# Retention values (first half) and attention values (second half) projected 512 columns at a time, with weights partly in the attention's buffers

## The chip, the cores and the metric

The kernel runs on one core of one Trainium2 chip. The metric is the device time of the core in microseconds (us), taken as the median of several runs of the compiled program. A second source is the profile of one execution: when each instruction of each engine started and ended, and what it waited for. The engines are TensorE (PE, with its weight loads as PEld), VectorE (DVE), ScalarE (ACT), GpSimd (POOL) and SyncE (SP), whose queue issues all the DMAs of this kernel.

## The reference, cut to what matters

One layer of a streaming encoder. Every row of x (2048 prompt rows and 64 sample rows, 1024 wide) is normalised and multiplied by one wide input weight, whose columns are cut into ten pieces:

```
h = rmsnorm(x, norm_g) @ w_in
qa, ka, va, za, qb, kb, vb, zb, ga, gb = jnp.split(h, _split_points(), axis=-1)
...
oa = diff_attn_prompt(qa, ka, va, lam, slopes)
ob, r_p = retention_prompt(qb, kb, vb, log_g)
...
oa = rmsnorm(oa, subln_g) * (1 - lam_init) * silu(za)
ob = rmsnorm(ob) * silu(zb)
m = sigmoid(ga + b_gate[0]) * (oa @ w_oa) + sigmoid(gb + b_gate[1]) * (ob @ w_ob)
y = x + m @ w_out
```

All of it is float32. `va` (attention values) and `vb` (retention values) are 512 columns each, as are `ka`, `qa`, `kb`, `qb`, `za`, `zb`; `ga` and `gb` are 1024 each. `va` is also an output. The sample rows attend to 4096 cached frames besides their own.

## The kernel before, in words

**Precision.** TensorE works on a rounded float32. Every operand is split into a high and a low part (`h` by an ACT cast, line 504, `l` by a subtraction, line 514), and a product is the sum of three matmuls: high by high, high by low, low by high (`mm_group`, line 554). So one 128-row tile of x against one piece of weights is 8 chunks of the contraction by 3 matmuls, 24 in all. The 64 sample rows go through line 550 with 16.

**Two halves.** The prompt's 2048 rows are worked on in two halves of 1024 rows (8 tiles of 128); the sample's 64 rows go with the first half. In each half a stream of projections runs, called W below (`w_stream`, from line 2072), over the column pieces in an order written out by hand. There are three forms:

- *Narrow* (`natural`, line 628): x is stationary, 256 columns of weights move. Two row tiles share one PSUM bank of 512 columns (tag `mm`, two banks). A 512-column piece takes two such passes, g = 0 and g = 1.
- *Wide* (`natural` with `wide`): x is stationary, 512 columns of weights move, one row tile fills a bank. Before the change the first half's `va`, `ka` and `qa` are wide, in this order.
- *Transposed* (`transposed`): weights are stationary and x moves. All of `qb`, `kb`, `za`, `zb`, `ga`, `gb`, in both halves.

In the first half before the change: wide `va`, `ka`, `qa`, then narrow `vb` (two passes), then the transposed pieces. In the second half (`ORD`, line 2237): narrow `va` g 0, `ka` g 0, `qa` g 0, a mark, `va` g 1, `ka` g 1, `qa` g 1, a mark, then narrow `vb` and the transposed pieces.

**Eviction.** `fin_va` (line 763) scales the bank by the rows' norms on ACT (line 786), splits it, and stores high part, low part and output. `fin_vb` (line 815) scales it on ACT (line 827) and stores it. `fin_qk` normalises, transposes (line 734) and stores queries and keys. All go to scratch in DRAM, from which attention and retention load them.

**Weight rooms.** A weight piece is loaded into one of three staging buffers (`ws`), cast and subtracted into two rooms, `wh` and `wl` (`w_room`, line 470; `w_piece`; `w_low`). Narrow pieces use the 12 `w` rooms, two each. Before the change, wide pass 0 (`va`) and wide pass 2 (`qa`) use the attention's buffers `K` and `V` (four of each; one `K` and one `V` hold two of a pass's eight pieces), and wide pass 1 (`ka`) uses the `w` rooms and the two `q` buffers. A room comes free when the last tile of its pass has used it.

**The attention side**, called Z below (`z_stream`): for each half and each of four heads, `load_head` takes `K` and `V` buffers (two of each per head in the first half, four of each in the second) and loads keys and values; `attn_head` and `qk_block` do the scores (lines 1052 and 1053), softmax, transposes (line 1160) and values (lines 1138 to 1140). After the first half's heads come the sample's attention (lines 1221 to 1420) and eight blocks of retention (lines 1486 to 1563); in the second half four blocks follow head 2 and four follow head 3.

**What sets the order.** The program is written by a planner: tasks with priorities and a model of each engine's time decide the order of instructions on PE, ACT, DVE and POOL, which is then fixed; the DMAs on SP are ordered by the framework. Z has priority, and W fills the time in which Z waits. Z of a half may start when the mark `kqv0` (then 0 or 1 for the half) is set: in the first half after the wide `qa`, in the second after `qa` g 0, so with only half of `va`. Heads 2 and 3 wait for `kqv1`.

**The output stage.** When Z is done, `out_prep` loads the branches' output weights, `zaT`, `oaT`, `zbT`, `obT` and gates for the first of eight groups, then for the next (`og_fin`, high and low parts by lines 1677 and 1680). When W is done, the output matmuls begin: eight groups of 8 tiles by 24 matmuls (`m_tile`, lines 1722 to 1724), then the last projection (line 1934), for which `b_prep` loads `w_out`.

Of the kernel before, what the change touches and what calls it, by code (L numbers as in the profile page):

```python
# [8 lines left out]
F32 = mybir.dt.float32  # L9
# [50 lines left out]
class Hybrid:  # L60
# [434 lines left out]
    def w_piece(self, wait):  # L495
# [9 lines left out]
        th = self.A(512, max(self.pe, t))  # L505
        return self.w_low(wide, n, st, h, l, th, tag, tags)

    def w_low(self, wide, n, st, h, l, t, tag, tags):
        th = t
        if n == 1:  # L510
            self.nc.vector.tensor_sub(l, st, h.bitcast(F32))
# [250 lines left out]

    def fin_va(self, g, nh=2):
        nc = self.nc
        ep = self.ep
        hs = slice(2 * g, 2 * g + nh)

        def fin(ps, r, nu, t0, t, bank="mm"):
            n, rt = 128 * nh * nu, r * nu
            rs, eps = yield from self.roots(t0)  # L770
            home = "ev" if nh < 4 or r < 128 else "ath" if t0 // 128 % 2 else "atl"
            yield from self.take(home)
            if nh == 4:
                yield from self.take("row")
                both = self.row("vhl").bitcast(F32R)
                hi, lo = both[:r, :512], both[:r, 512:]
            else:
                yield from self.take("thi")
                yield from self.take("tlo")
                hi = self.sb(ep, [128, 512], "thi", dt=F32R)[:r, :n]  # L780
                lo = self.sb(ep, [128, 512], "tlo", dt=F32R)[:r, :n]
            raw = self.sb(ep if home == "ev" else self.ap, [128, 512], home, "raw")[:r, :n]
            w = 128 * nh
# [6 lines left out]
            t1 = self.A(n, t2)  # L790
            nc.vector.tensor_sub(lo, raw, hi.bitcast(F32))
            t3 = self.V(n, t1)
            if t0 < T:
                dst = self.o["v_prompt"][0, 0, t0:t0 + rt, hs]
            else:
                dst = self.o["v_sample"][0, 0, :, hs]
            yield t1
            gsl = slice(256 * g, 256 * g + 128 * nh)
            th = self.rows_out(self.vN[0][t0:t0 + rt, gsl], hi.bitcast(F32), nu, nh << 16)
            if nh < 4:  # L800
                self.give("thi", th)
            yield t2
            td = self.rows_out(dst.rearrange("t h e -> t (h e)"), raw, nu, nh << 16)
            if t0 == T:
                td = self.st(self.vsN[:, gsl], raw, 1 << 16)
            self.give(home, td)
            yield t3
            tl = self.rows_out(self.vN[1][t0:t0 + rt, gsl], lo.bitcast(F32), nu, nh << 16)
            if nh < 4:
# [6 lines left out]
    def fin_vb(self, g):  # L816
        nc = self.nc
        ep = self.ep

        def fin(ps, r, nu, t0, t, bank="mm"):  # L820
            n, rt = 256 * nu, r * nu
            rs, eps = yield from self.roots(t0)
            yield from self.take("ev")
            raw = self.sb(ep, [128, 512], "ev", "raw")[:r, :n]
            for u in range(nu):
                sl = slice(256 * u, 256 * u + 256)
                nc.scalar.activation(raw[:, sl], ps[:, sl], AF.Identity, scale=rs[:r, u:u + 1])
                t = self.A(256, t, 60)
            self.give(bank, t)
            yield t  # L830
            self.give("ev", self.rows_out(self.vbN[t0:t0 + rt, 256 * g:256 * g + 256], raw, nu, 1 << 17))

# [125 lines left out]
    def load_head(self, half, h):  # L958
# [1113 lines left out]
    def w_stream(self):  # L2072
        self.wq = []
        qa, ka, va, za, qb, kb, vb, zb, ga, gb = range(0, 5120, 512)
        gb = 5120
        fva = [(va + 256 * g, lambda half, g=g, f=f: self.natural(half, self.fin_va(g), f))
               for g in range(2) for f in (True, False)]
        fva, fva0 = fva[1::2], fva[0]
# [8 lines left out]
        for g in range(2):  # L2087
            seq.append((vb + 256 * g, lambda half, g=g: self.natural(half, self.fin_vb(g))))
        for base, dst, n, sc in ((qb, self.qbT, 2, None), (kb, self.kbT, 2, KB_SCALE)):
# [9 lines left out]
        seqs = [f + seq for f in first]  # L2099
        self.order = [[(c[0], len(c) > 2) for c in q if c[0] is not None] for q in seqs]  # L2100
# [10 lines left out]
        for half in range(2):  # L2111
            for k, (c0, f, *_) in enumerate(seqs[half]):
                if c0 is None:
                    self.spawn(self.mark(f"{f}{half}"), 0)
                else:
                    yield from f(half)
                if half == 0 and c0 == vb + 256:
                    self.give("row", self.pe)
# [24 lines left out]
    def z_stream(self):  # L2143
        for half in range(2):
            yield lambda: f"kqv0{half}" in self.done
            if half == 0:
# [89 lines left out]

def ORD(va0, va, k, q, m0, m1):
    return [va0, k[0], q[0], m0, va[1], k[1], q[1], m1]

# [56 lines left out]
```

## Time and profile before

| | |
|---|---|
| median of 3 runs | 1945.42 us (1945.01 to 1947.52) |
| the profiled execution | 1945.82 us, span of its instructions 1944.0 us |
| TensorE clock granted, mean | 0.998 of full |
| PE, PEld busy | 1927.5 us, 1731.2 us |
| DVE, ACT, POOL busy | 1166.6 us, 964.9 us, 490.1 us |
| DMA | 303.32 MB, mean 156 GB/s |
| first half's wide and narrow passes | from the start to 230 us |
| attention scores, first half and second half | 189.8 to 388.1 us and 876.8 to 1441.7 us |
| last matmul of W, first of the output stage | about 1575 us |

The span is the time from the first to the last instruction; the execution's own time is 1.8 us more. A matmul's duration in the trace overlaps the next matmul's, so the rate of a run of matmuls is read from the distance of their starts: the chain of waits gives such runs as start, length and count. "Idle" stands in the trace for time in which an engine had nothing running, with what ended it.

### The profile page before, as it was taken

How to read it: one execution, taken by the hardware profiler on the slowest of the kernel's cores; microseconds unless marked ns; L12 is line 12 of the kernel's file. 1: busy time of each engine (PE TensorE's matmuls, PEld its weight loads, DVE VectorE, ACT ScalarE, POOL GpSimd, SP SyncE). 2: the span in 40 equal slices, each digit the busy share in tenths (PEclk: the TensorE clock that was granted, in tenths of full speed). 3: DMA queues.
4: the chain of work that ended last, by engine and by line, in shares of the span. 5: the costliest groups of instructions: out<-in, count | busy, mean ns of one | idle time of the engine just before them, and what ended most of it. 6: DMA issues, size and time to landing. Idle time of an engine off the chain costs nothing.

```text
span 1944.0 us, 33842 instructions
## 1 busy us (share of the span) xinstructions
PE 1927.5 (99%) x11984; PEld 1731.2 (89%) x11984; DVE 1166.6 (60%) x2798; ACT 964.9 (50%) x2072; POOL 490.1 (25%) x429
## 2 busy tenths in 40 slices
PE   9999999999999999999999999999999999999999
PEld 8779999999988899999998888888888889998887
DVE  6753777646666336648856757845773376545643
ACT  7443766544434235535765646544563445653321
POOL 4310112112122121211121111112113356543422
PEclk9999999999999999999999999999999999999999
DMA  7747454335566655654344253363133678866651
GB/s 235 240 151 199 143 143 132 106 102 156 163 192 187 166 148 168 202 183 141 112 120 128 76 146 96 99 185 116 63 99 108 190 229 259 264 196 189 190 151 65
DMA packets 372074, 303.32 MB, mean 156 GB/s; under 512 B 77440, under 2 KB 334720, under 8 KB 371904
## 3 DMA queue, kind: packets, MB, share of 16 engines
q1 hardware_dynamic: 371904, 301.16, 52.6%
q8 instruction: 94, 1.54, 0.4%
q14 instruction: 76, 0.62, 0.1%
HBM read 195.87 MB, written 100.14 MB: 152 GB/s over the span
## 4 chain that ended last, share of the span: by engine, by line
PE 88%; DVE 5%; DMA 3%; POOL 1%; issue 1%; ACT 1%; SPq 1%; DVEq 0%; POOLq 0%; ACTq 0%
PE mm L554 51%; PE mm L1934 4%; PE s L1052 3%; PE s L1053 3%; PE at L1160 3%; PE at L1934 2%; PE pv L1139 2%; PE pv L1140 2%; PE pv L1138 2%; PE s L1934 1%; PE s L1723 1%; PE s L1724 1%; PE pv L1521 1%; PE mm L1723 1%; PE s L1722 1%
## 5 line engine op out<-in xcount | busy, mean ns | idle before, releaser
L514 POOL TENSOR_TENSOR wl<-ws,wh 128x512 fp32r<-128x512 f32 x191 | 261.4, 1380 | 896.2 <-ACT wh L504 544.9
L554 PE MATMUL mm<-xh,wh 128*128 128x512 f32 (+2 forms) x1280 | 460.7, 360 | 0.0
L554 PE MATMUL mm<-xh,wl 128*128 128x512 f32 (+2 forms) x1280 | 452.7, 354 | 0.0
L554 PE MATMUL mm<-xl,wh 128*128 128x512 f32 (+2 forms) x1280 | 451.9, 353 | 0.0
L554 PEld LDWEIGHTS mm<-xh,wl 128*128 128x128 f32 x1280 | 241.0, 188 | 31.7
L554 PEld LDWEIGHTS mm<-xh,wh 128*128 128x128 f32 x1280 | 241.4, 189 | 29.1 <-issue 0.2
L554 PEld LDWEIGHTS mm<-xl,wh 128*128 128x128 f32 x1280 | 241.6, 189 | 27.8
L554 PE MATMUL mm<-wh,xh 128*128 128x256 f32 (+1 forms) x768 | 236.7, 308 | 0.0
L554 PE MATMUL mm<-wh,xl 128*128 128x256 f32 (+1 forms) x768 | 231.3, 301 | 0.0
L554 PE MATMUL mm<-wl,xh 128*128 128x256 f32 (+1 forms) x768 | 231.0, 301 | 0.0
L1175 DVE TENSOR_TENSOR atl<-at,ath 128x512 fp32r<-128x512 f32 (+1 forms) x144 | 93.7, 659 | 136.2 <-ACT ath L1173 136.1
L504 ACT CAST wh<-ws 128x512 fp32r<-128x512 f32 x192 | 117.0, 617 | 112.6 <-PE mm L554 90.3
L1091 ACT ACTIVATE row<-row,a_mx 128x1024 f32<-128x1024 f32 (+7 forms) x160 | 153.7, 962 | 24.5 <-DVE a_mx L1071 24.3
L554 PEld LDWEIGHTS mm<-wh,xh 128*128 128x128 f32 x768 | 146.3, 190 | 7.1 <-issue 0.5
L554 PEld LDWEIGHTS mm<-wl,xh 128*128 128x128 f32 x768 | 146.4, 191 | 6.7 <-issue 0.5
L554 PEld LDWEIGHTS mm<-wh,xl 128*128 128x128 f32 x768 | 146.3, 190 | 5.5
L865 DVE TENSOR_TENSOR ev<-mm,rsb 128x512 f32<-128x512 f32 x140 | 83.0, 593 | 112.8 <-PE mm L554 112.4
L1173 ACT CAST ath<-at 128x512 fp32r<-128x512 f32 (+1 forms) x144 | 78.7, 563 | 141.5 <-PE at L1160 138.4
L1061 DVE CUSTOM_DVE_ANT_0 row<-s,dfar 128x512 f32<-128x512 f32 (+2 forms) x192 | 118.2, 630 | 46.4 <-PE s L1053 45.9
L1052 PE MATMUL s<-K,q 128*128 128x512 f32 (+3 forms) x320 | 118.4, 374 | 0.7 <-DVE a_acc L1061 0.7
L1053 PE MATMUL s<-K,q 128*128 128x512 f32 (+3 forms) x320 | 115.2, 362 | 0.0
L1110 ACT ACTIVATE row<-row,a_w 128x1024 f32<-128x1024 f32 (+4 forms) x96 | 85.1, 898 | 34.4 <-DVE a_w L1105 31.2
(342 smaller groups left out, 4193.5 us busy)
## 6 DMA issues: line engine op xcount, KB each, us to landing
ws<-in_w_in_dram SPq DMA_DIRECT2D x192, 256.0 KB, 3.1
q<-qT SPq DMA_DIRECT2D x128, 128.0 KB, 3.0
V<-vN SPq DMA_DIRECT2D x24, 512.0 KB, 5.4
K<-kT SPq DMA_DIRECT2D x48, 256.0 KB, 4.3
a<-mT SPq DMA_DIRECT2D x34, 256.0 KB, 4.1
gt<-gaT SPq DMA_DIRECT2D x64, 132.0 KB, 3.2
gt<-gbT SPq DMA_DIRECT2D x64, 132.0 KB, 3.1
mT<-gt SPq DMA_DIRECT2D x64, 132.0 KB, 3.0
```

The source lines that it names most:

```text
L504: self.nc.scalar.copy(h, st)
L514: self.nc.gpsimd.tensor_sub(l, st, h.bitcast(F32))
L554: nc.tensor.matmul(ps, p, q, start=c == 0 and i == 0, stop=c == KC - 1 and i == 2)
L865: nc.vector.tensor_mul(ev, ps, rsb)
L1052: nc.tensor.matmul(ps, q1s, kk, start=True, stop=False)
L1053: nc.tensor.matmul(ps, q2s, kk, start=False, stop=True)
L1061: nc.vector.tensor_tensor_reduce(out=units[k0 // 1024][:, k0 % 1024:k0 % 1024 + n], in0=ps, in1=tab, scale=-SLOPES[h], scalar=3.0e38, op0= ...
L1091: nc.scalar.activation(u, u, AF.Exp, bias=mx, scale=-1.0, accum_out=lp[:, k:k + 1])
L1110: nc.scalar.activation(u1, u1, AF.Identity, scale=w[:, 1:2])
L1173: nc.scalar.copy(ah[:, :w], at[:, :w])
L1175: nc.vector.tensor_sub(al[:, :w], at[:, :w], ah[:, :w].bitcast(F32))
L1934: nc.tensor.matmul(q[b], u, v, start=fresh and c == 0 and m == 0, stop=c == 3 and m == 2, skip_group_check=True)
```

## The change

It makes the first half's `vb` one wide pass (wide pass 3) in place of two narrow ones, and the second half's `va` one wide pass (wide pass 4) in place of two. The second half's order becomes: wide `va`, a mark `v1`, `ka` g 0, `qa` g 0, the mark `kq01`, `ka` g 1, `qa` g 1, the mark `kq11`, narrow `vb`, the transposed pieces. The first half's order keeps its form, with wide `vb` in the place of the narrow one.

The eight weight pieces of wide pass 3 go to `w` rooms (pieces 0 to 3) and to `K` and `V` buffers (4 to 7, two of each); those of wide pass 4 to two `K` and two `V` (0 to 3) and to `w` rooms (4 to 7). Four subtractions of pass 3 (odd pieces) go from POOL to DVE. `load_head` waits for the values' own mark between the loads of keys and of values. `fin_va` and `fin_vb` evict a bank with one ACT instruction of 512 columns where two of 256 did it, and store 512 columns of 128 rows in one DMA where one of 256 columns for two tiles did it.

```
 def w_room
-        elif nw != 1:
+        elif nw in (0, 2) or (nw == 3 and q > 3) or (nw == 4 and q < 4):
             tags, pool, shape = ("K", "V"), self.ap, [128, 2, 512]
-        elif q < 6:
+        elif nw > 2 or q < 6:
             tags, pool, shape = ("w", "w"), self.wp, [128, 1, 512]
...
 def w_piece
-        return self.w_low(wide, n, st, h, l, th, tag, tags)
+        return self.w_low(wide, n == 1 or (nw in DLOW and wide and q % 2), st, h, l, th, tag, tags)
...
 def w_low
-        if n == 1:
+        if quick:
             self.nc.vector.tensor_sub(l, st, h.bitcast(F32))
...
 def fin_va
-            for u in range(nu):
-                sl = slice(w * u, w * u + w)
-                nc.scalar.activation(raw[:, sl], ps[:, sl], AF.Identity, scale=rs[:r, u:u + 1])
-                t2 = self.A(w, t, 90)
+            nc.scalar.activation(raw, ps, AF.Identity, scale=rs[:r, 0:1])
+            t2 = self.A(512, t, 90)
...
-            th = self.rows_out(self.vN[0][t0:t0 + rt, gsl], hi.bitcast(F32), nu, nh << 16)
+            th = self.st(self.vN[0][t0:t0 + r], hi.bitcast(F32), 1 << 18)
...
 def fin_vb
-                sl = slice(256 * u, 256 * u + 256)
+                sl = slice(256 * w * u, 256 * w * u + 256 * w)
...
 def load_head
                 ks[c][u] = k
+        yield from self.stored(f"v{half}")
         for u in range(nu):
...
 def head_in
-        k = f"kqv{h // 2}{half}"
+        yield from self.stored(f"kq{h // 2}{half}")
+
+    def stored(self, k):
         yield lambda: k in self.done
         yield self.marks[k] + 9000
...
 def w_stream
-        m0, m1 = (None, "kqv0"), (None, "kqv1")
-        wva = (va, lambda half: self.natural(half, self.fin_va(0, 4), True, True), True)
+        m0, m1, mv = (None, "kq0"), (None, "kq1"), (None, "v")
+        wva = (va, lambda half: self.natural(half, self.fin_va(half), half == 0, True), True)
+        wvb = (vb, lambda half: self.natural(half, self.fin_vb(2), False, True), True)
+        fvb = [(vb + 256 * g, lambda half, g=g: self.natural(half, self.fin_vb(1, g))) for g in range(2)]
...
-        first = ([wva, wk, wq, m0, m1], ORD(fva0, fva, fk, fq, m0, m1))
+        first = [wva, wk, wq, m0, m1, mv, wvb], ORD2(wva, fk, fq, m0, m1, mv)
...
-def ORD(va0, va, k, q, m0, m1):
-    return [va0, k[0], q[0], m0, va[1], k[1], q[1], m1]
+def ORD2(va, k, q, m0, m1, mv):
+    return [va, mv, k[0], q[0], m0, k[1], q[1], m1]
...
+DLOW = (3,)
```

More of the change, by code (lines that the diff above doesn't have):

```diff
@@ L505, in w_piece, with w_low @@
         th = self.A(512, max(self.pe, t))
-        return self.w_low(wide, n, st, h, l, th, tag, tags)
-    def w_low(self, wide, n, st, h, l, t, tag, tags):
+        return self.w_low(wide, n == 1 or (nw in DLOW and wide and q % 2), st, h, l, th, tag, tags)
+    def w_low(self, wide, quick, st, h, l, t, tag, tags):
         th = t
-        if n == 1:
+        if quick:
             self.nc.vector.tensor_sub(l, st, h.bitcast(F32))
@@ L761, in fin_qk, with fin_va @@
         return fin
-    def fin_va(self, g, nh=2):
+    def fin_va(self, half):
         nc = self.nc
         ep = self.ep
-        hs = slice(2 * g, 2 * g + nh)
         def fin(ps, r, nu, t0, t, bank="mm"):
-            n, rt = 128 * nh * nu, r * nu
             rs, eps = yield from self.roots(t0)
-            home = "ev" if nh < 4 or r < 128 else "ath" if t0 // 128 % 2 else "atl"
+            home = "ev" if half or r < 128 else "ath" if t0 // 128 % 2 else "atl"
             yield from self.take(home)
-            if nh == 4:
+            if half == 0:
                 yield from self.take("row")
@@ L814, in fin_va, with fin_vb @@
         return fin
-    def fin_vb(self, g):
+    def fin_vb(self, w, g=0):
         nc = self.nc
@@ L820, in fin @@
         def fin(ps, r, nu, t0, t, bank="mm"):
-            n, rt = 256 * nu, r * nu
+            n, rt = 256 * w * nu, r * nu
             rs, eps = yield from self.roots(t0)
@@ L825, in fin @@
             for u in range(nu):
-                sl = slice(256 * u, 256 * u + 256)
+                sl = slice(256 * w * u, 256 * w * u + 256 * w)
                 nc.scalar.activation(raw[:, sl], ps[:, sl], AF.Identity, scale=rs[:r, u:u + 1])
-                t = self.A(256, t, 60)
+                t = self.A(256 * w, t, 60)
             self.give(bank, t)
             yield t
-            self.give("ev", self.rows_out(self.vbN[t0:t0 + rt, 256 * g:256 * g + 256], raw, nu, 1 << 17))
+            self.give("ev", self.rows_out(self.vbN[t0:t0 + rt, 256 * g:256 * g + 256 * w], raw, nu, w << 17))
         return fin
@@ L2098, in w_stream @@
                             self.transposed(half, dst, 2 * g, final=fin)))
-        seqs = [f + seq for f in first]
+        seqs = [first[0] + seq, first[1] + fvb + seq]
         self.order = [[(c[0], len(c) > 2) for c in q if c[0] is not None] for q in seqs]
@@ L2116, in w_stream @@
                     yield from f(half)
-                if half == 0 and c0 == vb + 256:
+                if half == 0 and c0 == vb:
                     self.give("row", self.pe)
@@ L2144, in z_stream @@
         for half in range(2):
-            yield lambda: f"kqv0{half}" in self.done
+            yield lambda: f"kq0{half}" in self.done
             if half == 0:
```

31 lines of the change are left out of this document (12 added, 19 removed).

## The prediction

> **What bounds the kernel now.** I read the page first, then the chain of waits, then the attention's first and last instructions, then SP's timeline where the stages meet.
>
> ```profile
> span 1944.0 us, 33842 instructions
> ...
> PE 1927.5 (99%) x11984; PEld 1731.2 (89%) x11984; DVE 1166.6 (60%) x2798; ACT 964.9 (50%) x2072; POOL 490.1 (25%) x429
> ...
> PE   9999999999999999999999999999999999999999
> ...
> PE 88%; DVE 5%; DMA 3%; POOL 1%; issue 1%; ACT 1%; SPq 1%; DVEq 0%; POOLq 0%; ACTq 0%
> ```
>
> TensorE is busy 99% of the span, in every slice, and is 88% of the chain that ended last. So a nanosecond taken off its instructions comes off the time unless something new makes it wait; and a wait of Z costs nothing while W has matmuls to put in its place. Three questions follow: what the wide form saves on PE, what the seams around the changed passes cost, and whether W and Z still end in the right order. The profiled execution took 1945.82 us, 0.4 us above the median of 1945.42 us, and 1.8 us more than its span; I sum changes and apply them to the median.
>
> **What the wide form saves.** Matmul durations overlap, so I take the pitch (start to start) from unbroken runs in the chain: start, length, count.
>
> ```profile
> 88.56 5.54 PE mm L554 x24
> ...
> 151.02 5.58 PE mm L554 x24
> ...
> 158.44 3.73 PE mm L550 x16
> ...
> 167.36 10.78 PE mm L554 x90
> ...
> 849.68 8.64 PE mm L554 x72
> 858.76 18.19 PE mm L554 x150
> ...
> 1524.68 50.39 PE mm L554 x222
> ```
>
> The first two are wide passes of the first half: 5.54/24 = 230.8 ns and 5.58/24 = 232.5 ns for 512 columns. The runs at 167, 849 and 858 us are narrow passes: 119.8, 120.0 and 121.3 ns for 256 columns. The last is a transposed pass of 512 columns with nothing beside it: 227.0 ns. Two narrow matmuls cost 240 ns, one wide 230.8: 9.2 ns less per pair. Each half has 8 tiles by 8 chunks by 3 products, 192 pairs, so 384 pairs give 384 x 9.2 = 3.5 us. Bounds: with 232.5 ns against 240, 2.9 us; with 227.0 ns against 2 x 121.3, 6.0 us. I take 3.5, since the wide natural passes have the changed passes' own operands. The columns streamed stay the same; only a fixed part of each matmul is saved. The sample's tile (16 matmuls, 3.73 us wide) saves nothing, as the narrow pass's row shows, twice 1.87:
>
> ```profile
> 186.64 1.87 PE mm L550 x16
> ```
>
> The Trainium skill (TensorE: Matmul & The Clock Gate, "Back-to-back issue gap") gives a warm gap of columns/2.4 plus 2.5 ns; as an estimate from that page a pair would cost 218.3 against 215.8 ns, and the whole change would save 1.0 us. The rows above disagree (twice 119.8 against 230.8), and the measurement decides.
>
> Off the path: the same 16 weight pieces are loaded, cast and subtracted, four subtractions on DVE, and ACT evicts a bank with one instruction for two. ACT at 50% and DVE at 60% are not the bound, and SP issues the same number of DMAs.
>
> **The seam in the first half.** Pieces 4 to 7 of the new `vb` pass need rooms in which the `qa` pass still has its weights, and ACT has a hole there:
>
> ```profile
> L514 POOL TENSOR_TENSOR wl<-ws,wh 128x512 fp32r<-128x512 f32 x191 | 261.4, 1380 | 896.2 <-ACT wh L504 544.9 <-PE mm L554 111.6 <-PE s L1053 102.5
> ...
> L504 ACT CAST wh<-ws 128x512 fp32r<-128x512 f32 x192 | 117.0, 617 | 112.6 <-PE mm L554 90.3 <-DMA ws<-in_w_in_dram 17.1 <-DMA V<-vN 1.7
> ...
> ws<-in_w_in_dram SPq DMA_DIRECT2D x192, 256.0 KB, 3.1
> ```
>
> ```profile
> 184.98 0.47 ACT L744 ACTIVATE thi<-tp,gq 128x256 fp32r<-128x256 f32 x1 [9.55 <-DMA qT<-thi]
> 185.35 0.83 ACT L827 ACTIVATE raw<-mm,rs 128x256 f32<-128x256 f32 x2
> ```
>
> The `qa` pass's last group runs 158.44 to 162.17, and its rooms come free with every second of its 8 chunks, the first at about 159.4. Piece 4 is then cast (0.62) and subtracted on POOL (1.38), ready at 161.4. With three staging buffers, piece 7's load (3.1) starts when piece 4 is done, so it is there at 164.5, cast by 165.1 and subtracted on DVE by about 166. The first wide tile starts at 162.6 and comes to chunk 4 at 165.4, chunk 7 at 167.4: covered by 1.4 us, if ACT is free. Queued behind piece 7's cast on ACT are the evictions of the banks, for which PE would wait. The second price is the bank: ACT waited 9.55 us for a DMA before 184.98, with the evictions behind it. Wide tile 3 ends at 162.6 + 3 x 5.54 = 179.2, and tile 5 wants its bank at 184.8; after 185.4 ACT needs about 0.8 us more, so PE would wait 1.4 us where narrow got by. A gain here has no reason in the trace; between 0 and 1.4 + 2.6 = 4.0 (piece 7's load and cast late by one load less its cover, added) I take 0.6, since ACT's order will not be quite the same.
>
> **Where attention starts.**
>
> ```profile
> L1052 PE MATMUL s<-K,q x96: 221/338/796, 189.8 to 388.1; 128*128 128x512 f32 x40, 128*128 128x256 f32 x24, 128*128 128x384 f32 x24, 128*128 128x128 f32 x8
> ```
>
> ```profile
> L1052 PE MATMUL s<-K,q x224: 221/393/481, 876.8 to 1441.7; 128*128 128x512 f32 x76, 128*128 128x256 f32 x20, 128*128 128x384 f32 x12, 128*128 128x128 f32 x4
> ```
>
> ```profile
> 223.66 0.31 PE L1052 MATMUL s<-K,q 128*128 128x128 f32 x1
> ```
>
> ```profile
> L550 PE MATMUL mm<-wh,xs x32: 277/338/400, 104.9 to 229.8; 128*128 128x512 f32 x16, 128*128 128x256 f32 x16
> ```
>
> ```profile
> 837.75 2.39 SPq L135 DMA_DIRECT2D K<-kT  x2
> ```
>
> In the first half head 0 starts at 189.8 as before. Two `K` buffers of head 1 (223.66, the first score of 128 columns again) will hold `vb` weights until that pass's sample tile, which ends at about 230 now, so head 1 starts some 10 us later. PE loses nothing, for W fills the place; a load that comes later than the planner thinks would stop PE in order, which the seam's bound leaves room for. The second half's `va` gives its rooms back before `ka` begins, and head 0's keys of that half load at 837.75, after `ka`: no wait there. The new mark for the values comes no later than the keys' mark in either half, so its wait is nothing.
>
> In the second half the run of 150 projection matmuls at 858.76, just before the first score at 876.8, shows that Z waits for its mark there. The mark now comes after the whole of `va`: 192 x 230.8 ns = 44.3 us where g 0 took 192 x 120 ns = 23.0 us, so 21.3 us later, less 1.8 us saved in the first half: 19.5 us. W is that much further ahead, so PE's work is the same. But Z ends 19.5 us nearer to W's end.
>
> **The end of W.** This is the rule of the program that speaks against the change: the output stage's inputs are prepared while only W runs.
>
> ```profile
> 1529.93 1.77 SPq L135 DMA_DIRECT2D wst<-in_w_o_diff_dram  x4
> ...
> 1533.64 0.43 SPq L135 DMA_DIRECT2D z<-zaT  x1
> ...
> 1563.77 0.37 SPq L135 DMA_DIRECT2D z<-zaT  x1
> ...
> 1571.56 0.42 SPq L135 DMA_DIRECT2D z<-zbT  x1
> 1578.13 1.76 SPq L135 DMA_DIRECT2D wst<-in_w_out_dram  x4
> ```
>
> ```profile
> L1680 DVE TENSOR_TENSOR ogl<-on,ogh x8: 432/434/982, 1542.0 to 1551.6; 128x264 fp32r<-128x264 f32 x8
> ```
>
> Preparation starts at 1529.93, 5 us after Z's last matmul (1524.68, where the run of 222 W matmuls begins); group 0's operands are ready at 1552.0, 22.1 us on, and SP's loads go on until 1572. W ends at 1575.1. After the change preparation starts at 1549.4, group 0 is ready at 1571.5, and W ends at 1575.1 - 3.5 + 0.6 = 1572.2: just covered. Group 1's first five pairs were issued from 1563.77 to 1572, so now from 1583.3 to 1591.5; 8.4 us from a load to its operand (1533.64 to 1542.0 for group 0's first) make it 1591.7 to 1599.9. Group 1 is wanted a group later:
>
> ```profile
> 1574.90:1598.00 23.10, 22.31 (x181) 21.93 (x180) 17.93 (x28) 11.20 (x28) 14.82 (x16) 1.00 0.64 198
> ...
> 1621.00:1644.00 23.00, 20.22 (x142) 19.81 (x141) 13.87 (x27) 13.88 (x34) 11.84 (x13) 0.85 0.79 245
> ```
>
> That is 1572.2 + 23.1 = 1595.3: up to 4.6 us late if SP keeps its order, on time if SP lets them pass loads that are not yet needed. I take 0.6 for the forecast and keep the rest for a rival.
>
> **Sum:** -3.5 + 0.6 + 0.6 = -2.3 us, so 1943.1 us; with this case's bounds 1941.0 to 1945.4.
>
> **Rival 1, slower: preparation takes the place of the cover.** If SP serves the later loads in the old order, the last three pairs of group 1, issued after those five, come 2.4 us later still (6 issues of 0.4): PE waits 4.6 + 2.4 = 7.0 us. There is a second price, for the clock:
>
> ```profile
> 1624.69 0.28 PE L1724 MATMUL mm<-ogh,woq 128*128 128x264 f32 x1
> 1626.05 0.39 PE L1722 MATMUL s<-ogh,woq 128*128 128x264 f32 x1 [1.08 <-ACT ogh L1677]
> 1628.14 0.59 PE L1723 MATMUL s<-ogl,woq 128*128 128x264 f32 x1 [1.70 <-DVE ogl L1680]
> ```
>
> ```profile
> 1628.73 0.22 PE s L1724
> ...
> 1634.01 0.22 PE s L1724
> ```
>
> After 1.08 and 1.70 us of idle the pitch was 0.22 us for 25 matmuls, where the groups' mean is 0.12: 2.5 us lost, and the mean clock of that stretch was 0.85. The Trainium skill (the same page, "Part 1: The HAM clock gate") says that idle windows of about 3.4 us bring the clock to half; here two gaps of 2.8 us together were followed by it. Together 9.5 us, so 1945.4 - 2.9 + 9.5 = 1952.0 us; with 4.6 alone and no dip, 1947.1. It decides once Z ends more than 14.9 us later: 1572.0 + 8.4 = 1580.4 is when the fifth pair is ready now, 1595.3 when it is wanted. For it: the sum of 19.5. Against it: SP's order is not the program's, and Z might run faster with fewer projections beside it.
>
> **Rival 2, faster: the output stage's own gaps go.** The 2.8 us of idle and 2.5 us of slow clock at 1625 to 1634 hang on what meets there; moved, they may vanish: 1945.4 - 2.9 - 5.3 = 1937.2 us. For it: one place holds the largest stall of the execution. Against: Rival 1 makes the same place worse.
>
> **Rival 3: the saving is eaten at the seam,** that is, the change brings nothing: with 3.1 us of waits, 1945.4 - 3.5 + 3.1 = 1945.0 us. For it: ACT's 9.55 us hole; against: the next tile's slack of 1.4 us.
>
> **How the numbers follow.** About 0.2% (3.9 us) is what a measurement of this kernel can tell from no change: faster is below 1941.5, slower above 1949.3. The forecast has 0.48 (0.20 of it below 1941.5, since the pitch's bound of 6.0 us and a free output stage reach there), Rival 1 0.27 (0.20 above 1949.3), Rival 2 0.15, Rival 3 0.10. So faster 0.35, same 0.28 + 0.07 + 0.10 = 0.45, slower 0.20. The range 1938 to 1952 leaves out the lower end of Rival 2 and the upper of Rival 1, under 2 in 10; the forecast's own is 1941.0 to 1945.4.
>
> **What would show it.** Right: wide `vb` and `va` runs at 230 to 231 ns in the chain; first score of the second half near 896 us; the pure W run at the end near 28 us; output matmuls from about 1572. Wrong: a pitch of 235 ns or more (no saving); PE idle at 162 to 190 us above 1.5 us (the seam); idle plus slow clock between 1590 and 1645 clearly above the 5.3 us of now (Rival 1) or near none (Rival 2).

## The result and the profile after

The changed kernel takes 1959.0 us in the median, against 1946.36 us for the kernel before, run beside it. The ratio is 1.0061, with an interval from 1.0044 to 1.0078: about 12 us slower. Both medians are of six runs, one of which, on each side, took far longer (3161.18 us at a granted clock of 0.555, and 2340.97 us); the ratio leaves these two out. The forecast was 1943.1 us with a range from 1938 to 1952, so even the range missed it.

The profiled execution took 1959.97 us, its span is 1958.2 us, and that span is 14.2 us longer than before's. The same rows of the page as were shown of before:

```profile
span 1958.2 us, 33031 instructions
...
PE 1929.8 (99%) x11584; PEld 1715.1 (88%) x11584; DVE 1160.4 (59%) x2801; ACT 964.1 (49%) x2054; POOL 482.8 (25%) x425
...
PE   9998999999999999999999999999999999999999
...
PE 88%; DMA 4%; DVE 2%; ACT 2%; issue 1%; POOL 1%; SPq 1%; POOLq 0%; ACTq 0%; DVEq 0%
```

PE has 400 matmuls fewer and is busy for 2.3 us more. The one new thing to see is the 8 in the fourth slice of PE, between about 147 and 196 us, and DMA at 4% of the chain in place of 3%. Tables by stage show it better. Each row gives the stretch and its length, then the busy time of PE, PEld, DVE, ACT and POOL, and at the end the granted clock, the DMA share and GB/s. First before, then after:

```profile
160.00:190.00 30.00, 30.00 (x245) 29.13 (x243) 6.54 (x16) 9.34 (x23) 1.90 (x2) 1.00 0.93 241
...
230.00:300.00 70.00, 70.00 (x452) 64.88 (x451) 52.29 (x165) 45.60 (x106) 16.32 (x14) 1.00 0.53 148
...
700.00:760.00 60.00, 60.00 (x408) 55.92 (x406) 29.40 (x60) 25.10 (x51) 13.98 (x10) 1.00 0.59 175
```

```profile
160.00:190.00 30.00, 24.45 (x102) 18.98 (x101) 14.46 (x31) 12.99 (x26) 4.65 (x4) 0.89 0.74 202
...
230.00:300.00 70.00, 67.44 (x416) 61.34 (x416) 48.94 (x159) 44.78 (x106) 14.03 (x12) 0.98 0.67 171
...
700.00:760.00 60.00, 57.82 (x360) 52.71 (x359) 15.49 (x31) 17.39 (x35) 17.74 (x14) 0.97 0.63 176
```

In three stretches where PE never paused it now does, for 5.55, 2.56 and 2.18 us, and in each the clock was lower too.

**The stop at 178 us.** The chain of waits, with start, length and what ran; then the rows of ACT, PE and SP at that place, where the brackets give the idle time and what ended it:

```profile
173.13 0.32 ACT sq L693
173.45 8.15 DMA vbN<-raw
...
181.62 0.63 ACT raw L696
...
182.27 0.69 ACT raw L821
182.96 0.59 ACT xroot L384
...
183.57 0.70 DVE xroot L390
...
184.32 1.11 PE tp L734 x4
...
185.43 4.15 PE mm L554 x12
```

```profile
181.62 0.62 ACT L696 COPY raw<-up 64x512 f32<-64x512 f32 x1 [7.88 <-DMA vbN<-raw]
```

```profile
184.32 1.11 PE L734 MATMUL tp<-ident,raw 128*128 128x128 f32 x4 [5.55 <-DVE xroot L390]
```

```profile
169.28 2.46 SPq L135 DMA_DIRECT2D K<-kT  x4
171.78 1.57 SPq L135 DMA_DIRECT2D V<-vN  x2
173.45 9.87 SPq L140 DMA_DIRECT2D vbN<-raw  x2
```

Read it from the end. PE's transposes of line 734 wait for a PSUM bank of the tag `tp`. That bank is held by the step that makes the row norms for the transposed pieces (`x_root`: a matmul of line 377, ACT lines 384 to 386, DVE line 390). The step's ACT instruction stands behind line 696 in ACT's order, and line 696 waits 7.88 us for an `ev` buffer: the first tile of the wide `vb` pass was evicted into it, and its store landed 8.15 us after it was issued. The store stands behind the loads of the first head, four of `K` and two of `V`. Then the 12 matmuls after the stop took 4.15 us, 346 ns each, where a wide one takes 232 ns.

**The second head.** The first rows are PE's, the others SP's:

```profile
251.45 0.36 PE L1049 MATMUL s<-K,q 128*128 128x256 f32 x1 [1.46 <-DMA q<-qT]
252.48 0.36 PE L1050 MATMUL s<-K,q 128*128 128x256 f32 x1 [0.68 <-DMA q<-qT]
```

```profile
235.17 0.42 SPq L135 DMA_DIRECT2D V<-vN  x1
...
236.76 0.42 SPq L135 DMA_DIRECT2D V<-vN  x1
237.24 2.59 SPq L135 DMA_DIRECT2D K<-kT  x4
...
241.14 4.69 SPq L135 DMA_DIRECT2D q<-qT  x4
```

Head 1 starts at 237.2 us (223.7 before). Its keys were issued from 219.3 us on, into the buffers of head 0; its values (the first two rows) and the keys of head 2 (the third) had to wait for the rooms with `vb` weights, whose last tile ends at about 236.5 us. The queries of head 1 issued behind them landed 7.1 to 9.6 us after their issue and came late for the scores.

**What came as forecast.** The pitches in the chain, and the first score of the second half from PE's timeline:

```profile
149.92 5.58 PE mm L554 x24
...
806.60 5.56 PE mm L554 x24
...
849.21 8.63 PE mm L554 x72
...
1544.33 40.18 PE mm L554 x177
```

```profile
911.19 0.39 PE L1049 MATMUL s<-K,q 128*128 128x512 f32 x1
```

In the second half the wide matmul takes 5.56/24 = 231.7 ns and two narrow ones 2 x 8.63/72 = 239.7 ns. The saving of 8.0 ns by 384 pairs is 3.1 us. The last run with W alone starts at 1544.33, 19.7 us later than before (1524.68), and lasts 40 us.

**An account of PE's time.** To put numbers on all stops at once I took, for each PE matmul, the distance from its start to the next start less the median distance of its kind (by the shapes of its two operands), and added up what is above zero. Gaps, waits and slow clock all count. Before, the sum is 62.8 us; after, it is 80.7 us, 17.9 more. The span grew by 14.2 us, so what is left, -3.7 us, is the gain in pitch. Where the 17.9 us lie: 60 to 300 us +12.7 (6.3 to 19.0; of it 160 to 190 us +8.8 and 240 to 300 us +4.5), 300 to 700 us -2.8, 700 to 900 us +4.1, the output matmuls from 1575 to 1705 us +4.9, the rest about -1.

### The profile page after: what moved, and what is told of

Its sections match the earlier page's. It is cut to its first block, busy times and chain, and to the rows that moved or that the text cites. A ratio compares the mean times of both kernels' runs of the same rounds, so it can differ in the third digit from the quotient of the medians.

```text
span 1958.2 us, 33031 instructions
## 1 busy us (share of the span) xinstructions
PE 1929.8 (99%) x11584; PEld 1715.1 (88%) x11584; DVE 1160.4 (59%) x2801; ACT 964.1 (49%) x2054; POOL 482.8 (25%) x425
## 3 DMA queue, kind: packets, MB, share of 16 engines
q8 instruction: 91, 1.49, 0.3%
## 4 chain that ended last, share of the span: by engine, by line
PE 88%; DMA 4%; DVE 2%; ACT 2%; issue 1%; POOL 1%; SPq 1%; POOLq 0%; ACTq 0%; DVEq 0%
PE mm L554 51%; PE mm L1931 4%; PE s L1049 3%; PE s L1050 3%; PE at L1157 3%; PE at L1931 2%; PE pv L1136 2%; PE pv L1137 2%; PE pv L1135 2%; PE mm L1719 1%; PE mm L1720 1%; PE mm L1721 1%; PE s L1931 1%; PE s L1720 1%; PE s L1721 1%
## 5 line engine op out<-in xcount | busy, mean ns | idle before, releaser
L554 PE MATMUL mm<-wh,xh 128*128 128x256 f32 (+1 forms) x640 | 215.7, 337 | 0.4 <-ACT raw L781 0.4
L554 PE MATMUL mm<-wl,xh 128*128 128x256 f32 (+1 forms) x640 | 209.8, 328 | 0.9 <-POOL wl L514 0.9
L554 PE MATMUL mm<-wh,xl 128*128 128x256 f32 (+1 forms) x640 | 210.0, 328 | 0.0
L554 PEld LDWEIGHTS mm<-wl,xh 128*128 128x128 f32 x640 | 122.1, 191 | 12.3 <-POOL wl L514 1.1
L554 PEld LDWEIGHTS mm<-wh,xh 128*128 128x128 f32 x640 | 122.0, 191 | 12.3 <-ACT raw L781 1.1
L554 PEld LDWEIGHTS mm<-wh,xl 128*128 128x128 f32 x640 | 121.8, 190 | 11.2
L1110 DVE SCALAR_TENSOR_TENSOR row<-row,a_w 128x1024 f32<-128x1024 f32 (+4 forms) x96 | 103.9, 1092 | 8.6 <-ACT row L1107 8.6
```

The source lines that it names most:

```text
L554: nc.tensor.matmul(ps, p, q, start=c == 0 and i == 0, stop=c == KC - 1 and i == 2)
L1110: nc.vector.scalar_tensor_tensor(out=u0, in0=u0, scalar=w[:, 0:1], in1=u1, op0=ALU.mult, op1=ALU.add)
```

## The experiments

My theory after the two traces: the gain in pitch is there, and the loss is made in the first half, where the wide `vb` pass meets the heads' loads in two places (its stores and the `ev` buffers, its weights in `K` and `V`). The norm's step came in as a third after e6 to e8. The first rival: the loss comes from the end, where Z ends later and the output stage's preparation has less cover. The second: the wide pass itself is slower, or the new order of the second half is.

| kernel | median us | ratio to before, 95% interval | span - 1944.0 | stops - 62.8 | rest | stops 60 to 300 us |
|---|---|---|---|---|---|---|
| before | 1944.25 to 1946.36 | 1 | 0 | 0 | 0 | 6.3 |
| after | 1959.0 | 1.0061 [1.0044, 1.0078] | +14.2 | +17.9 | -3.7 | 19.0 |
| e1 first half only | 1960.63 | 1.0078 [1.0064, 1.0092] | +13.4 | +15.5 | -2.1 | 17.7 |
| e2 second half only | 1945.75 | 0.9999 [0.999, 1.0008] | +0.1 | +2.2 | -2.1 | 6.4 |
| e3 late mark | 1954.7 | 1.0054 [1.004, 1.0068] | +8.6 | +9.0 | -0.4 | 6.3 |
| e4 other buffers | 1956.81 | 1.0057 [1.0044, 1.007] | +8.1 | +11.6 | -3.5 | 16.1 |
| e5 later head loads | 1952.18 | 1.0039 [1.0025, 1.0054] | +6.4 | +10.4 | -4.0 | 12.3 |
| e6 other rooms | 1951.7 | 1.0035 [1.0023, 1.0047] | +3.6 | +7.5 | -3.9 | 12.2 |
| e7 rooms and buffers | 1950.06 | 1.0025 [1.0014, 1.0036] | +1.5 | +5.3 | -3.8 | 12.1 |
| e8 e7, first half only | 1950.15 | 1.0026 [1.0017, 1.0036] | +5.6 | +7.5 | -1.9 | 12.2 |
| e9 e7, late norm step | 1945.86 | 1.0006 [0.9997, 1.0014] | -2.6 | +1.6 | -4.2 | 7.0 |
| e10 e7, spread norm steps | 1945.06 | 1.0005 [0.9996, 1.0014] | +0.8 | +4.5 | -3.7 | 7.3 |
| e11 e8, late norm step | 1951.04 | 1.0033 [1.0021, 1.0045] | +5.3 | +7.0 | -1.7 | 7.0 |
| e12 after, late norm step | 1954.4 | 1.0049 [1.0035, 1.0063] | +8.2 | +11.4 | -3.2 | 16.4 |

The first row's medians are those of the runs beside which the others were taken. The four columns on the right are of one profiled execution each, which lies up to 3 us from the median. "Rest" is span less stops: -3.2 to -4.2 us in all kernels with both halves wide, -1.7 to -2.1 with one half, -0.4 with none. So the gain in pitch is there, and about as large as forecast. It is a remainder, though, and moves by some 2 us with the way in which kinds are told apart: with the matmul's line added to the shapes it is -5.6 us for the changed kernel.

**e1: only the first half's wide pass.** The kernel before with `vb` wide in the first half, its rooms and subtractions as in the change; the second half is untouched.

```
-        elif nw != 1:
+        elif nw in (0, 2) or (nw == 3 and q > 3):
...
+        first = ([wva, wk, wq, m0, m1, wvb], ORD(fva0, fva, fk, fq, m0, m1))
```

> Only the first half's vb is one wide pass; the second half keeps the narrow va and its early mark. Theory A (the loss arises in the first half: K and V loads for the heads hold up the store of vb's first tile, ACT waits for that buffer, PE stops for 5.7 us and runs on a slower clock, and head 1's loads come late at 249 us): 1946.4 - 1.8 + 8.8 + 4.5 = about 1958 us. Theory B (the loss arises in the output stage, because Z ends 20 us later): about 1944.6 us. If each has its share, A's part shows here: the stretch 160 to 190 us has about 9 us of stalls.

Measured: 1.0078, about 15 us slower than before and no better than the whole change, with PE idle 5.26 us before line 734 at the same place:

```profile
160.00:190.00 30.00, 24.74 (x106) 19.21 (x105) 14.89 (x33) 13.59 (x28) 5.25 (x4) 0.94 0.73 201
...
230.00:300.00 70.00, 68.02 (x419) 61.81 (x418) 49.35 (x162) 45.50 (x107) 14.05 (x12) 0.98 0.66 171
```

W's cover for the preparation (the time in which PE runs W alone at the end) is 50.2 us here, as before, and the output matmuls take 196.3 us (before 197.8). So the end has no part in this loss: the first half's wide pass makes it all. Not all of it lies in the first half: of its stops 11.4 us more than before lie between 60 and 300 us, and 6.6 between 700 and 900.

**e2: only the second half's wide pass.** The changed kernel with `vb` narrow in the first half.

```
-        first = [wva, wk, wq, m0, m1, mv, wvb], ORD2(wva, fk, fq, m0, m1, mv)
+        first = [wva, wk, wq, m0, m1, mv] + fvb, ORD2(wva, fk, fq, m0, m1, mv)
...
```

> Only the second half's va is one wide pass; the first half keeps narrow vb in the w rooms. Theory A: 1946.4 - 1.8 = 1944.6 us, with no stall at 160 to 300 us. Theory B: 1944.6 + 4.4 (output stage of the profile after, 202.2 us against 197.8 for its first part) = 1949.0 us, and Z's last matmul at about 1544.

Measured: no difference (0.9999). Here the second half's attention starts at 900.7 us, 23.9 later than before, but Z ends at 1533.6, only 9.2 later: on the way it gains 14.7 us. W alone has 40 us at the end, as in the changed kernel. The 2.1 us that the pass saves don't show in the time, since the stops are 2.2 us more.

**e3: only the later mark.** The kernel before with both narrow `va` passes ahead of the mark. No matmul changes its form; Z starts later.

```
-    return [va0, k[0], q[0], m0, va[1], k[1], q[1], m1]
+    return [va0, va[1], k[0], q[0], m0, k[1], q[1], m1]
```

> The kernel before with no wide pass added: only the second half's order is changed, both narrow va passes ahead of ka, qa and the mark. PE's work is the same. Theory B: Z ends about 21 us later than before and the output stage costs 4.4 us more, about 1950.8 us. Theory A: no change, 1946.4 us; then the later end of Z is harmless and the output stage of the profile after was longer for another reason.

Measured: 1.0054. Z ends at 1545.8, W alone has 28.5 us, and the output matmuls take 206.7 us, 8.9 more than before. That is about twice the 4.4 us that was expected. They wait for their operands:

```profile
1574.00:1597.00 23.00, 19.82 (x147) 19.31 (x146) 18.11 (x34) 12.19 (x32) 12.20 (x15) 0.93 0.87 268
1597.00:1620.00 23.00, 18.98 (x126) 17.96 (x125) 17.30 (x30) 15.75 (x40) 15.52 (x18) 0.85 0.89 277
```

```profile
1592.68 0.39 PE L1722 MATMUL mm<-ogh,woh 128*128 128x264 f32 x1 [2.77 <-DVE gt L1742]
...
1606.27 0.39 PE L1723 MATMUL s<-ogl,woq 128*128 128x264 f32 x1 [1.48 <-DVE ogl L1680]
```

That is Rival 1 of the prediction, by itself, at a cover of 28.5 us. The changed kernel never gets there: its cover is 40.0 us. That isn't because its W is late, for e2 has the same cover with W's end at 1574 us. PE's order is fixed when the program is written, and in both 177 matmuls of W stand behind Z's last one (222 before, 126 in e3).

**e4: other buffers for the evictions.** The changed kernel, with the first four tiles of the wide `vb` evicted into `ath` and `atl`, which attention has not begun to use, in place of `ev`.

```
...
+            home = "ev" if w < 2 or t0 >= 512 else "ath" if t0 // 128 % 2 else "atl"
...
```

> The kernel after with one thing changed: the first half's vb tiles 0 to 3 are evicted into the attention's ath and atl buffers (not used before the first transposes at about 200 us) in place of the ev buffers that the sample's queries need. The order on PE up to the first score stays. Theory A: the 5.7 us stop at 178 us and its slow clock go, about 8 us less than after, 1950 us. Rival (PE stopped because weights in the K and V rooms or the loads themselves come late): the stop stays, 1958 us.

Measured: the stop at 178 is gone (PE busy 30.00 of 30.00 us from 160 to 190), and the time is hardly less than the changed kernel's (1.0057 after 1.0061). A new stop of 7.07 us stands at 239.7. ACT's row, then SP's:

```profile
244.70 0.37 ACT L898 COPY r_o<-pv 128x256 f32<-128x256 f32 x1 [9.39 <-DMA oaT<-r_o]
```

```profile
229.66 1.05 SPq L135 DMA_DIRECT2D V<-vN  x2
230.75 4.28 SPq L135 DMA_DIRECT2D K<-kT  x4
...
236.40 3.09 SPq L135 DMA_DIRECT2D q<-qT  x4
240.04 0.34 SPq L140 DMA_DIRECT2D oaT<-r_o  x1
```

It is the same figure with other actors. The values of head 1 and the keys of head 2, late because their rooms held `vb` weights, and then head 1's queries are ahead of a store of attention's output; ACT waits for its buffer, and PE for ACT.

**e5: later head loads.** The changed kernel, with the loads of the first half's heads held back for 21 us of the planner's time after the mark, in place of 9.

```
-        yield self.marks[k] + 9000
+        yield self.marks[k] + (21000 if k[-1] == "0" else 9000)
```

> The kernel after with the first half's loads of keys, values and queries allowed 12 us later (21 us after their marks in place of 9). Theory A (the burst of K and V loads at 169 to 173 us holds up the store of vb's first tile, and so the sample's queries): the burst comes after that store, the stop at 178 us goes, and the time falls by 5 to 9 us against after, to about 1951 us; the later start of Z costs nothing, since W fills the place. Rival (PE's order alone makes the stop): it stays at 5 to 6 us, 1958 us.

Measured: 1.0039, about 4 us less than the changed kernel by the ratios. No stop from 160 to 190 us, with the norm's step still at 168 to 176 us: the store of the first `vb` tile is now issued ahead of the loads and lands after 3.43 us. In the second head PE still waits 2.51 and 0.82 us, before its scores at 242.25 and 243.48.

**e6: other rooms.** The changed kernel, with pieces 4 to 7 of wide `vb` in four of the ten `row` buffers, so that `K` and `V` are free for the heads.

```
-        elif nw in (0, 2) or (nw == 3 and q > 3) or (nw == 4 and q < 4):
+        elif nw == 3 and q > 3:
+            yield from self.take("row")
+            r = self.row("whl").bitcast(F32R)
+            return [r[:, :512], r[:, 512:]], ("row",)
+        elif nw in (0, 2) or (nw == 4 and q < 4):
```

> The kernel after with pieces 4 to 7 of the first half's wide vb in four of the ten row buffers in place of two K and two V buffers, so that head 1's keys and values can be loaded early again. If the late loads of head 1 (235 to 248 us) make the stop at 249 us, that stop goes (4 us); the stop at 178 us stays or grows, since the early burst is twice as long (8 K and 4 V loads): 1954 us. If the rooms are not what delays them, 1958 us.

**e7: both.** e6 with e4's buffers.

> Both changes: row buffers for the weights (e6) and the attention's ath and atl buffers for the first four evictions of vb (e4). If the loss of the first half is made of the two stops that these take away, both go and the kernel is where the wide passes should bring it: 1958 - 8.8 - 4.5 = about 1945 us, no slower than before by more than the output stage's 1 to 4 us. If either stop comes back in another place, 1952 us or more.

**e8: both, first half only.** e1 with e4's buffers and e6's rooms.

> As the last one, but the second half as before (narrow va, early mark): Z ends as in the kernel before, so the output stage has its full lead. If the stops are gone: 1945.2 - 1.8 = 1943.4 us, faster than both kernels. If they come back: 1950 us or more.

Measured: 1.0035, 1.0025 and 1.0026. By the ratios 5 and 7 us of the changed kernel's 12 come back, and 10 of e1's 15. All stops from 160 to 300 us are gone in all three, but a new one came before that. In e7, PE's timeline and then pieces of the chain:

```profile
128.91 0.50 PE L558 MATMUL mm<-wh,xh 128*128 128x512 f32 x1 [1.94 <-ACT raw L700]
137.61 0.46 PE L738 MATMUL tp<-ident,raw 64*128 64x64 f32 x4 [1.57 <-DVE tlo L749]
```

```profile
127.01 0.32 ACT xroot L384
...
128.39 0.48 ACT raw L700
...
138.07 8.72 PE mm L558 x30
```

The norm's steps stood at 168 to 175 us in the changed kernel. They are released by a count of weight loads, and these come earlier now that rooms are free earlier. So they now stand inside the wide query pass. At 127 us ACT's instructions of the norm's step for the sample lie ahead of the copy of line 700 that PE waits for; at 136 two groups of transposes stand back to back in the new order, and the second waits for the first's `tp` bank. From 60 to 160 us the stops are 9.0 us (before 3.4). So e6 alone took both old stops away, against its expectation that the one at 178 would stay: the heads' loads are still ahead of a store of `vb` there (issued at 182.8 us, landed 9.4 us later), but the norm's step no longer stands behind it. Whether e4's buffers are needed beside e6's rooms was not tried by itself; e6 and e7 lie within each other's intervals. Since e6, e7 and e8 had this stop in common, I had not yet shown what the wide pass costs without one.

**e9: the norm's steps late.** e7, with the two large steps waiting for 38 loads.

```
-        yield lambda: self.wloads > (32, 36)[seg] if half == 0 else self.spread_ok
+        yield lambda: self.wloads > (37, 37)[seg] if half == 0 else self.spread_ok
```

> As e7 (weights of the wide retention values in row buffers, evictions of its first tiles in ath and atl), with one condition changed: the two steps that make the prompt's row norms for the transposed pieces (PE L377, ACT L384) wait until 38 weight pieces are loaded instead of 33 and 37, so that they come after the wide pass's start and not at 127 us, where e7 stopped for 2.10 and 1.73 us and ran 9.0 us over its pitches between 60 and 160 us (before: 3.4). Theory (every loss of the first half is a stop where some eviction or load meets the wide passes; nothing else is wrong with the wide pass): the stops at 127 and 136 go and nothing takes their place, so e7's 1950.1 falls by about 5.5 us to 1944 to 1946, about the time before. Rival (any wide pass here has too little slack in ACT and in the banks, so a stop that is taken away comes again somewhere else before 300 us): 1949 to 1953 with a new stop of over 2 us.

**e10: the steps spread.** The same with (36, 37).

> As e9, but the first of the two steps may go when 37 pieces are loaded, and the second when 38 are: in the program's order the first then stands inside the wide query pass, 45 matmuls behind the sample's step, and the second some 300 later. Theory (a stop arises only where the step meets a late eviction): the first step costs at most the 2 us of one stop, 1944 to 1948. Rival (no slack in any wide pass): 1949 to 1953, with stops near 127 us as in e7.

Measured: 1945.86 and 1945.06 us, no difference from before. In e9 the stretches are whole again, although head 1 starts at 242.8 us, later than in the changed kernel:

```profile
160.00:190.00 30.00, 30.00 (x139) 24.28 (x138) 5.87 (x12) 7.12 (x13) 0.00 (x0) 1.00 0.95 254
...
230.00:300.00 70.00, 70.00 (x445) 64.21 (x444) 56.52 (x182) 48.45 (x108) 15.04 (x12) 1.00 0.56 155
...
700.00:760.00 60.00, 60.00 (x355) 53.67 (x354) 26.65 (x49) 28.19 (x56) 18.35 (x14) 1.00 0.72 209
```

With the three meetings undone, the 12 us are back within the interval. e9's profiled execution is 2.6 us shorter than before's; its median is not. So no kernel's median shows the saving in pitch: e2, e9 and e10 have 1.6 to 4.5 us more of stops than before, which use it up.

**e11: e8 with e9's step.**

> As e8 (only the first half's retention values wide, odd weights in row buffers, early evictions in ath and atl; the second half as in the kernel before), with the norm's two steps of e9 waiting for 38 loads. Theory (all of the first half's loss is clashes, and the second half gains and loses nothing in sum): the 5.6 us that e8 loses at 127 to 136 go, so 1950.2 falls to 1944 to 1946, and to 1943 if the 1.8 us of saved pitch show in full. Rival (the first half's wide pass costs something beside its stops): 1948 or more.

Measured: 1951.04 us, 5 us above what the theory allows. The stops at 127 and 136 went (60 to 300 us: 7.0), but others came: 1.47 us before 341.6 and 1.61 before 415.0 (in e9 it is 0.64 and 1.49 at the same places), and above all in the stretch in which retention, the loads of the second half's x and the narrow passes meet:

```profile
760.00:900.00 140.00, 136.66 (x1128) 134.12 (x1129) 81.83 (x223) 67.92 (x165) 29.25 (x22) 1.00 0.62 189
```

So the theory holds for the first 300 us only. The time is the one that the rival expected, but not for its reason: e11's loss is made of stops too (+7.0), in another place. A stop taken away in this schedule may come again elsewhere. Why e9, with the second half wide, has PE idle for only 1.0 us in that stretch (e11 3.3) was not tried and stays open.

**e12: the changed kernel with e9's step alone.**

> The changed kernel with only the norm's two steps moved behind 38 loads; weights in K and V and evictions in the ev buffers stay. In the changed kernel these steps stand at 168 to 175 us, just ahead of the 5.72 us stop at 178. Theory (the stop at 178 comes from a store of the retention values that lies behind the first head's loads, the later ones from the second head's late loads, and the steps only tighten the same place): 1954 to 1960, with a stop of 3 to 8 us between 160 and 260 us left. Rival (the steps were the culprit from the start, since moving them took 5 us off e7): 1947 to 1951 and no stop of over 2 us before 300 us.

Measured: 1954.4 us, within what the theory expected. The ratio, 1.0049, is 2 us less than the changed kernel's and within its interval. Its stretches, and ACT's two long waits:

```profile
160.00:190.00 30.00, 30.00 (x143) 24.30 (x141) 13.59 (x44) 14.15 (x37) 4.29 (x3) 1.00 0.85 241
...
230.00:300.00 70.00, 63.56 (x388) 57.25 (x387) 45.66 (x150) 41.24 (x96) 8.52 (x8) 0.95 0.60 155
```

```profile
180.92 0.47 ACT L744 ACTIVATE thi<-tp,gq 128x256 fp32r<-128x256 f32 x1 [7.12 <-DMA qT<-thi]
...
244.33 0.37 ACT L897 COPY r_o<-pv 128x256 f32<-128x256 f32 x1 [9.51 <-DMA oaT<-r_o]
```

ACT stands idle for 7.12 us before 181 and PE loses nothing; ACT stands idle for 9.51 us before 244 and PE loses 4.61 us. The difference is what PE's next instructions need: W's matmuls with their own banks at 181, a result of ACT at 244. The step alone was not the culprit, but in the changed kernel it was what turned ACT's wait at 178 into PE's. The stop at 178 is gone with another buffer (e4), with later loads (e5) and with a later step (e12), each by itself: it took all three to make it.

## Why the prediction was wrong

**The saving on PE: right.** Forecast 3.5 us; 3.1 us by the pitches of the chain, 3.7 by the account, and about half of it with one half wide.

**The seam in the first half: this step failed.** It forecast 0.6 us, at most 4.0, and by the account the changed kernel lost 8.8 us more than before from 160 to 190 us alone (12.7 from 60 to 300). Even with every term at its worst bound (2.9 us saved, 4.0 at the seam, 4.6 at the output stage) the prediction's sum comes to 1951.1 us; the bounds that it gave for the forecast, 1941.0 to 1945.4, are narrower than that. Nor do its figures give the 2.6 us in the seam's bound: one load less its cover, 3.1 - 1.4, is 1.7 us. The place was the right one: ACT's hole of 9.55 us with the evictions behind it, and "PE idle at 162 to 190 us above 1.5 us" as the sign of an error. The reasoning took the next bank of W's tiles as the only thing that PE could want from ACT, and gave it 1.4 us. But it had not asked what else goes through ACT behind the waiting instruction. That was the norm's step, which holds a `tp` bank. Before the change its two large parts ran outside this stretch (PE line 377 at 122.1 and 197.1 us); after it the step stands at 168 to 175, since the program releases it by a count of weight loads. So a wait of 8 us on ACT became 5.55 us on PE, and the clock's loss came on top.

**Head 1: "PE loses nothing" failed.** The start came 13.5 us later, near the 10 forecast, but the reason was another: the keys, which the step had waiting for the `vb` weights, took head 0's buffers, and it was the values that waited. The step did name a load that comes later than planned, and left it to the seam's bound. Late loads don't only make their own head late: they stand ahead of queries and of stores on the same queue, and with the slow clock that cost 4.5 us from 240 to 300. A late start by itself is free, as the step claimed: in e9 head 1 starts at 242.8 and no stop follows.

**Where attention starts in the second half, and where Z ends: right in one number, by luck.** The forecast had the first score at 896 us and Z's end 19.5 us later; measured are 911.2 and 19.7. But e2, without the first half's loss, has 23.9 us at the start and 9.2 at the end. Z gains 14.7 us in the second half, and the first half's loss happens to fill the place. What the step was for, how much nearer Z comes to W's end, was wrong: 10.2 us in place of 19.5. It took the time from Z's start to its end as unchanged, but between them stand 147 matmuls of W fewer than before (1911 in place of 2058), in e2 as in the changed kernel.

**The end of W: forecast 1572.2 and a cover of 28 us; measured 1584.5 and 40 us.** W ended 9.4 us later than before because it had lost that much in the stops. The output matmuls take 202.2 us (197.8 before), with 4.9 us more stops, the largest 2.53 us. How much of it is cover stays open: kernels with the same 40 us of cover have from 197.4 (e4) to 202.2 us.

**The rivals.** Rival 1 named a real mechanism with nearly the right price: 9.5 us forecast, 8.9 measured in e3 at 28.5 us of cover. It isn't what made this change slow: against W's end Z came 10.2 us nearer (cover 50.2 to 40.0 us), short of the 14.9 from which the rival was to decide. Rival 2 did not happen. Rival 3, the saving eaten at the seam, had the right place and a price of 3.1 us in place of 8.8; I had set the price equal to the gain, and nothing in the trace said that it would stop there.

**What was not foreseen:** the stops from 700 to 900 us, 4.1 us more than before in the changed kernel (6.6 in e1, 0.8 in e8). In the first 60 us of that stretch PE waited 1.27 us for the squares of the second half's x, whose eight loads were issued from 708.2 us on (695.7 before). No run was made for this alone; in e9 PE is never idle from 700 to 760 us.

## What to carry to other kernels

When a change makes one engine wait longer, list everything that stands behind the waiting instruction in that engine's order, with the banks and buffers that it holds, and not only the work of the changed pass. A burst of loads on one queue is a wait for each store issued behind it, and for whatever needs that store's buffer: so the price of a room that comes free later is to be looked for at the stores of others. In a schedule written by a planner, look for steps that are released by a count or a clock of the planner, since a change elsewhere moves them; and add up stops over the pitch per stage, for the gain and the loss are then seen apart.

## What the runs showed of the hardware

- A store's landing depends on what is queued ahead of it. The row of the view of DMA issues gives size and median time to landing:

```profile
vbN<-raw SPq DMA_DIRECT2D x16, 256.0 KB, 2.2
```

  The store at 173.45 took 8.15 us. Ahead of it four loads of 256 KB and two of 512 KB had been issued within 4.2 us; 2.1 MB at that stretch's 202 GB/s take 10.4 us. The Trainium skill (DMA: Bandwidth & Descriptors, "Queues, rings and completion order") says that each DMA engine takes a ring's descriptors in order; the 8.15 us beside 2.2 agree with that.
- A stop can cost more than its length. After 5.55 us of idle PE the next 12 wide matmuls took 346 ns each in place of 232, 1.4 us more, and the mean clock from 160 to 190 us was 0.89; by the account that stretch lost 8.8 us. The Trainium skill (TensorE: Matmul & The Clock Gate, "Why this matters for your kernels") warns of a lower clock after idle gaps of more than about 3 us. This gap agrees. But in e7 a lower clock also followed gaps of 1.94 and 1.57 us, 7 us apart: the 30 wide matmuls from 138.07 took 8.72 us, 291 ns each. Nor is the longest gap what decides: in the changed kernel the mean clock was 0.83 from 725 to 735 us around a gap of 1.27 us, and in e11 it was 1.00 from 410 to 425 us around one of 1.61 us. What does decide stays open.
